# A weight's high part multiplies high and low activations in one 512-column product, and two sums are added afterwards

## The chip, the cores and the metric

The kernel runs on one core of a Trainium2 chip. The metric is the device time of one execution in microseconds (us), lower is better; three executions of the kernel before took 2799.14 to 2809.85 us, median 2800.09 us. TensorE (PE) multiplies matrices into PSUM, VectorE (DVE) and ScalarE (ACT) do the elementwise work and read PSUM, GpSimd (POOL) does a few small operations, and SyncE (SP) issues the loads of the weights. Each engine takes its instructions from a queue of its own, in order.

## The reference

The program is a network of four layers on 256 tokens of width 1024, in 32-bit floats. The first block has two layers, each a mixer, a cross attention to 256 memory tokens and an expert layer (a product key search over two tables of 16384 rows); the second block has two layers, each an attention mixer and a gated feed-forward layer. What matters here are the products of the normalised activations with a weight:

```python
h = h + short_conv_pool_mixer(hn, even_w_in[j], ...)                  # u, gate_c, gate_b, pv = split(hn @ w_in)
q = (h @ wq).reshape(B_, S_, X_HEADS, X_HEAD_DIM)                       # cross attention, both layers
k, v = jnp.split(mem_n @ wkv, 2, axis=-1)
q = (xb @ wq).reshape(PEER_BLOCK, PEER_HEADS, 2, PEER_HALF)             # the experts' query
act = jax.nn.gelu(jnp.einsum('td,ted->te', xb, u[eid]))                 # the experts' first table, u
...
    gu = h @ w_gate_up                                                  # feed-forward, D_FF = 2816
    gate, up = gu[..., :D_FF], gu[..., D_FF:]
    return (jax.nn.silu(gate) * up) @ w_down
```

## The kernel before

**High and low parts.** Every product is made of three. A weight block arrives as 128 x 1024 floats in a tile `raw` (512 KB, one load by SP). ACT copies it, rounded, into `hi` (L114), and DVE subtracts to get `lo` (L117). Activations are split in the same way: `norm_T` fills `xh` and `xl`, each 128 x 8 x 256 (feature chunk by token), on ACT (L281) and DVE (L282). A product is then hi*xh + hi*xl + lo*xh, three matmuls into one PSUM sum (`mm3`, L152 to L154).

**Two forms.** `rows` has the weight as the streamed operand, 512 columns at a time, and sums in the four banks `a0` to `a3`. `columns` has the weight as the loaded operand: for each of 8 feature chunks it loads hi, streams 256 columns of xh, loads hi again, streams 256 columns of xl, loads lo, streams 256 columns of xh. That is 24 matmuls of 256 columns for one block of 128 outputs, in the lower half of one of two banks, `mm0` and `mm1`, which alternate. A bank is used again two blocks later, and has to have been read by then.

**Where `columns` runs.** The experts' first table (names `pu`, 256 blocks, not touched by the change); the experts' queries (`pwq`, 32); the feed-forward's gate and up (`fgu`, 88, that is 44 pairs); queries and keys of the cross attention (`xwq`, 16, and `xwk`, 16); the first mixer (`ein`, 16); the second mixer (`oiq` 6, `ohf` 4, `ohq` 4, `oql` 8); the third (`eqk` 8) and the fourth (`oqk` 10). Nearly always ACT reads the bank and writes the result to SBUF with one instruction, which also applies a scale or a function (Silu at L1311, Sigmoid at L799, scale 1/16 at L419). For `up`, DVE multiplies the bank with the gate straight from PSUM (L1314).

**What sets the order.** The order of each engine's instructions is that of the code. `w` hands out the split block number i, and before it does so it issues the splits up to block i + 2 (three tiles `hi` and three `lo`) and the loads up to block i + 6 (four tiles `raw`). So in the queue of ACT the copy `hi` of block i + 2 stands ahead of what ACT does with the result of block i, and `hi` of block i + 3 stands behind it; likewise `lo` on DVE.

**Names in the diff.** `memory` makes the keys and values of the cross attention and keeps the split memory (`kept`) in DRAM for the second layer; `weave` and `fill` place steps of other work between the blocks, in a fixed rhythm.

Of the kernel before, what the change touches and what calls it, by code (L numbers as in the profile page):

```python
# [20 lines left out]
F32 = mybir.dt.float32  # L21
F32R = mybir.dt.float32r
# [4 lines left out]
OP = mybir.AluOpType  # L27
# [47 lines left out]
class Program:  # L75
    RAW, HL, AHEAD, AHEAD_D = 4, 3, 3, 4

    def __init__(self, nc, tc, ins, out, order, start, stop):
        self.nc, self.tc, self.ins, self.out = nc, tc, ins, out
        self.order = order  # L80
        self.second = None
        self.n_mm = self.n_tp = 0
        self.given2 = [NOTHING] * 5
        self.kept = [NOTHING] * 2
# [71 lines left out]
    def columns(self, ps, name, j, xT, k_n=8):  # L156

        hi, lo = self.w(name, j, 128 * k_n)
        for k in range(k_n):
            s = slice(k * 128, (k + 1) * 128)  # L160
            self.mm3(ps, hi[:, s], lo[:, s], xT[0][:, k, :], xT[1][:, k, :], k == 0, k == k_n - 1)

    def rows(self, name, ks, xT, acc, gain=None):

        ks = list(ks)
        cut = len(ks) - 2
        for k in ks[:cut]:
# [59 lines left out]
    def norm_T(self, src, gain, xn=None, fill=0):  # L227

        hi, lo = [self.act.tile([128, 8, 256], F32R, name=f"x{i}", bufs=1) for i in "hl"]
        done, self.normed = self.normed, 1  # L230
        if xn is not None:
            for _ in self.norm_steps(src, gain, hi, lo, self.ss, xn, self.r, done):
                self.fill(fill)
            return hi, lo
# [5 lines left out]
        return hi, lo  # L240

# [48 lines left out]
    def memory(self, l, pool):  # L290
        nc = self.nc
        mT = [pool.tile([128, 8, 256], F32R, name=f"m{i}") for i in "hl"]
        if l == 0:
# [14 lines left out]
            for k in range(8):  # L308
# [4 lines left out]
                if k % 2:  # L313
                    yield
            self.kept = [self.dram.tile([128, 8, 256], F32, name=f"kept{i}") for i in range(2)]
            for to, m in zip(self.kept, mT):
                nc.gpsimd.dma_start(to, m.bitcast(F32))
        else:
            for m, kept in zip(mT, self.kept):
                nc.gpsimd.dma_start(m.bitcast(F32), kept)  # L320
            yield
# [25 lines left out]
    def conv_pool(self, pool):  # L347
# [18 lines left out]
        for g in range(4):  # L366
            pv = pool.tile([128, 16 + 256], F32, name="pv", bufs=2)
            nc.vector.memset(pv[:, :16], 0.0)
            ps = self.ps_mm()[:, :256]
            self.columns(ps, "ein", 12 + g, xT)  # L370
            nc.scalar.activation(pv[:, 16:], ps, AF.Copy)
            s = pv
# [11 lines left out]
            u = pool.tile([128, 256], F32, name="u", bufs=2)  # L384
            ps = self.ps_mm()[:, :256]
            self.columns(ps, "ein", g, xT)
            nc.scalar.activation(u, ps, AF.Copy)
            yield
# [21 lines left out]
    def xattn(self, l, pool):  # L410
# [101 lines left out]
    def peer(self, l):  # L512
        nc, tc = self.nc, self.tc
        with tc.tile_pool(name=f"peer{l}", bufs=1) as pg:
# [24 lines left out]
            for j in range(16):  # L539
                ps = self.ps_mm()[:, :256]  # L540
# [11 lines left out]
            acc = self.accs()  # L552
            wT = [self.act.tile([128, 8, 256], F32R, name=f"x{i}", bufs=1) for i in "hl"]
            yield from weave(self.peer_down(l, A, wT, acc, 0), self.peer_weigh(l, A, iota, slot, gT, 1), 0.55)
# [161 lines left out]
    def odd_mixer(self, pool):  # L716
# [28 lines left out]
        for j in range(6):  # L745
            ps = self.ps_mm()[:, :256]
            self.columns(ps, "oiq", j, xT)
            nc.scalar.activation(ikw if j == 0 else iqT[:, j - 1, :] if j < 5 else ckvT, ps, AF.Copy)
            if j == 0:
# [43 lines left out]
    def odd_columns(self, pool, xT, H, qlT, lb):  # L793
        nc, v = self.nc, self.nc.vector
        f = H["lf"]
        for j in range(4):
            ps = self.ps_mm()[:, :256]
            self.columns(ps, "ohf", j, xT)
            nc.scalar.activation(f[:, j, :], ps, AF.Sigmoid)  # L799
            v.tensor_scalar(f[:, j, :], f[:, j, :], lb[:, 1, j:j + 1], lb[:, 0, j:j + 1], op0=OP.mult, op1=OP.add)  # L800
# [3 lines left out]
        for j in range(4):  # L804
            ps = self.ps_mm()[:, :256]
            self.columns(ps, "ohq", j, xT)
            nc.scalar.activation(H["hq"][:, j, :], ps, AF.Copy)
            yield
        for name, func in (("hg", AF.Silu), ("hi", AF.Copy)):
# [14 lines left out]
            for j in range(8):  # L824
                ps = self.ps_mm()[:, :256]
                self.columns(ps, "oql", j, xT)
                nc.scalar.activation(qlT[:, j, :], ps, AF.Copy, scale=128.0 ** -0.5)
                yield
# [242 lines left out]
    def even_mixer(self, pool):  # L1071
# [45 lines left out]
        for j in range(8):  # L1117
            ps = self.ps_mm()[:, :256]
            self.columns(ps, "eqk", j, xT)
            nc.scalar.activation((qB if j < 4 else kB)[:, j % 4, :], ps, AF.Copy, scale=0.125 if j < 4 else 1.0)  # L1120
            if j == 0:
# [135 lines left out]
    def window_mixer(self, pool):  # L1257
# [11 lines left out]
        def gemm():  # L1269
            for j in range(10):  # L1270
                ps = self.ps_mm()[:, :256]
                self.columns(ps, "oqk", j, xT)
                nc.scalar.activation((vT, kT)[j] if j < 2 else qT[:, j - 2, :], ps, AF.Copy, scale=1.0 if j < 2 else 0.125)
                if j == 1:
# [27 lines left out]
    def ffn(self, l, pool):  # L1302
# [4 lines left out]
        for j in range(22):  # L1307
            ps = self.ps_mm()[:, :256]
# [3 lines left out]
            ps = self.ps_mm()[:, :256]  # L1312
# [307 lines left out]
```

## Time and profile before

| | |
|---|---|
| median of three executions | 2800.09 us (2799.14 to 2809.85) |
| the profiled execution | 2809.7 us, of it the span 2807.9 us |
| PE busy | 2739.6 us, 98% of the span |
| weight loads on PE | 2465.9 us |
| DVE busy | 1992.6 us, 71% |
| ACT busy | 1346.5 us, 48% |
| chain of work that ended last | PE 92%, DVE 4%, ACT 2% |
| mean rate of DMA | 165 GB/s |

Busy time is read against the span. A matmul's row starts where its columns begin to stream, and its end is modelled and lies beyond the next one's start; so the pace of matmuls is read from start to start, and the idle time in a row tells only of gaps that are longer than that overlap.

### The profile page before, as it was taken

What the parts mean: (1) busy time and instruction counts of PE and PEld (TensorE: products, weight loads), DVE (VectorE), ACT (ScalarE), POOL (GpSimd) and SP (SyncE); (2) the same over time, 40 slices, a digit from 0 to 9 for tenths busy, and PEclk for the clock granted to TensorE, in tenths of its full rate; (3) what the DMA queues carried; (4) which work ended last, traced back from release to release, by engine and by line L of the source; (5) the groups of instructions that cost most, each with busy time, mean ns of one, the idle gap of its engine ahead of it and who ended that gap; (6) DMA issues with size and microseconds to landing.
All of it is one profiled execution on the core that took longest, in us unless ns stands there. A gap on an engine that the chain in (4) does not pass through costs nothing.

```text
span 2807.9 us, 50252 instructions
## 1 busy us (share of the span) xinstructions
PE 2739.6 (98%) x20160; PEld 2465.9 (88%) x20160; DVE 1992.6 (71%) x3692; ACT 1346.5 (48%) x2272; POOL 66.6 (2%) x109
## 2 busy tenths in 40 slices
PE   8999999999999999999999999999999999999998
PEld 7889999998888888978999999888887769977997
DVE  7457898898996566755779889899656545556654
ACT  5455444434444555455544433444455545445543
POOL 2000000000000010100000000000000000000000
PEclk9999999999999999999999999999999989999999
DMA  6645555544555565344555544555555415552454
GB/s 226 212 133 163 186 176 165 167 155 160 166 166 188 194 184 182 123 129 142 166 181 180 173 160 155 163 169 166 187 193 167 165 53 179 183 166 89 158 182 148
DMA packets 127338, 463.32 MB, mean 165 GB/s; under 512 B 14912, under 2 KB 15192, under 8 KB 126336
## 3 DMA queue, kind: packets, MB, share of 16 engines
q1 hardware_dynamic: 122688, 445.31, 48.9%
q0 software_dynamic: 3776, 14.40, 1.7%
q8 instruction: 158, 2.59, 0.4%
q14 instruction: 76, 0.62, 0.1%
q10 hardware_dynamic: 640, 0.40, 0.0%
HBM read 456.64 MB, written 3.34 MB: 164 GB/s over the span
## 4 chain that ended last, share of the span: by engine, by line
PE 92%; DVE 4%; ACT 2%; issue 2%; DMA 1%; POOL 0%; POOLq 0%; DVEq 0%; ACTq 0%; SPq 0%
PE mm L152 16%; PE mm L154 16%; PE mm L153 15%; PE a L152 12%; PE a L154 12%; PE a L153 12%; PE tp L681 3%; DVE lo L117 1%; PE tp L486 1%; PE a L1232 1%; PE a L439 1%; ACT hi L114 1%; PE tp L535 1%; PE a L427 0%; PE a L970 0%
## 5 line engine op out<-in xcount | busy, mean ns | idle before, releaser
L117 DVE TENSOR_TENSOR lo<-raw,hi 128x1024 fp32r<-128x1024 f32 (+2 forms) x847 | 1033.1, 1222 | 614.3 <-ACT hi L114 610.8
L114 ACT ACTIVATE hi<-raw 128x1024 fp32r<-128x1024 f32 (+2 forms) x847 | 890.4, 1051 | 531.3 <-PE a L154 502.1
L152 PE MATMUL mm<-xh,hi 128*128 128x256 f32 x3584 | 1030.3, 287 | 3.3 <-DVE xl L282 2.4
L154 PE MATMUL mm<-xh,lo 128*128 128x256 f32 x3584 | 1019.8, 285 | 7.2 <-DVE lo L117 7.2
L153 PE MATMUL mm<-xl,hi 128*128 128x256 f32 x3584 | 1019.3, 284 | 0.9 <-DVE xl L282 0.9
L154 PEld LDWEIGHTS mm<-xh,lo 128*128 128x128 f32 x3584 | 691.1, 193 | 9.9 <-DVE lo L117 9.9
L152 PEld LDWEIGHTS mm<-xh,hi 128*128 128x128 f32 x3584 | 691.4, 193 | 8.7 <-DVE xl L282 3.8
L153 PEld LDWEIGHTS mm<-xl,hi 128*128 128x128 f32 x3584 | 691.4, 193 | 1.1 <-DVE xl L282 1.1
L152 PE MATMUL a<-hi,xh 128*128 128x512 f32 x1072 | 424.8, 396 | 1.6 <-ACT xh L273 1.6
L154 PE MATMUL a<-hi,xl 128*128 128x512 f32 x1072 | 418.6, 390 | 0.0
L153 PE MATMUL a<-lo,xh 128*128 128x512 f32 x1072 | 417.4, 389 | 0.0
L561 ACT ACTIVATE A<-mm 128x256 f32<-128x256 f32 x256 | 104.5, 408 | 445.7 <-PE mm L154 445.7
L154 PEld LDWEIGHTS a<-hi,xl 128*128 128x128 f32 x1072 | 201.2, 188 | 43.5 <-DVE xl L274 0.3
L152 PEld LDWEIGHTS a<-hi,xh 128*128 128x128 f32 x1072 | 201.5, 188 | 41.4 <-ACT xh L273 2.0
L153 PEld LDWEIGHTS a<-lo,xh 128*128 128x128 f32 x1072 | 201.7, 188 | 40.1
L673 DVE TENSOR_TENSOR go<-o,gT 128x512 bf16<-128x512 bf16 x384 | 140.3, 421 | 4.4
L681 PEld LDWEIGHTS <-o 128*128 128x128 bf16 x3072 | 96.7, 98 | 19.5 <-issue 16.7
L681 PE MATMUL tp<-go,o 128*128 128x64 bf16 x3072 | 111.9, 194 | 0.0
L274 DVE TENSOR_TENSOR xl<-A,xh 128x256 fp32r<-128x256 f32 x256 | 106.6, 418 | 2.0 <-ACT xh L273 2.0
L273 ACT ACTIVATE xh<-A 128x256 fp32r<-128x256 f32 x256 | 106.0, 416 | 0.0
L686 DVE TENSOR_TENSOR A<-tp,A 128x512 f32<-128x512 f32 x128 | 87.7, 685 | 0.0
L668 DVE TENSOR_TENSOR o<-iota,slot 128x1024 bf16<-128x1024 bf16 x128 | 87.6, 684 | 0.0
(463 smaller groups left out, 2548.0 us busy)
## 6 DMA issues: line engine op xcount, KB each, us to landing
raw<-pu SPq DMA_DIRECT2D x256, 512.0 KB, 3.7
raw<-pv SPq DMA_DIRECT2D x256, 512.0 KB, 4.3
raw<-fgu SPq DMA_DIRECT2D x88, 512.0 KB, 3.3
raw<-fdown SPq DMA_DIRECT2D x44, 512.0 KB, 3.4
raw<-pwq SPq DMA_DIRECT2D x32, 512.0 KB, 3.8
raw<-ein SPq DMA_DIRECT2D x16, 512.0 KB, 5.7
raw<-eout SPq DMA_DIRECT2D x16, 512.0 KB, 3.6
raw<-xwk SPq DMA_DIRECT2D x16, 512.0 KB, 4.3
```

The costliest lines, as they stand in the source:

```text
L114: self.nc.scalar.activation(hi, raw, AF.Copy)
L117: self.nc.vector.tensor_tensor(lo, raw, hi.bitcast(F32), OP.subtract)
L152: mm(out, ah, bh, start=start, stop=False)
L153: mm(out, ah, bl, start=False, stop=False)
L154: mm(out, al, bh, start=False, stop=stop)
L273: self.nc.scalar.activation(hi, src, AF.Copy)
L274: self.nc.vector.tensor_tensor(lo, src, hi.bitcast(F32), OP.subtract)
L561: self.nc.scalar.activation(A[:, c // 2, :, c % 2], ps, AF.Gelu_apprx_tanh)
L668: v.tensor_tensor(o2, iota[:, None].to_broadcast([128, 8, 64, 2]), slot[:, 1, t, None].to_broadcast([128, 8, 64, 2]), OP.is_equal)
L673: v.tensor_tensor(go[:, k], o1, gT[:, k, t, None].to_broadcast([128, 8, 32, 2]), OP.mult)
L681: nc.tensor.matmul(ps[:, j, :], o2[:, j].rearrange("p n two -> p (n two)"), go[:, k, j].rearrange("p n two -> p (n two)"), start=k == 0, s ...
L686: v.tensor_tensor(a, prod.pop(i).rearrange("p t (c two) -> p t c two", two=2), a, OP.mult)
```

## The change

A new helper, `columns_to`, takes the place of `columns` and the ACT instruction behind it at twelve places in the code, 200 blocks in all. The high and the low activations now lie side by side in one tile (`xhl`, `mhl`: chunk, part, token), so that the loaded hi streams 512 columns, [xh | xl], into a whole bank: hi*xh in the lower half, hi*xl in the upper. Then lo streams the 256 columns of xh into the lower half. There are 16 matmuls for a block in place of 24, with as many columns streamed. The halves are added outside PE: ACT copies the upper half to SBUF, DVE adds the lower half to it, and where a function or a scale is wanted ACT applies it in a third instruction. The second half of the gate pair (`up`) is now written to a tile by the same two instructions, and multiplied from there. The experts' first table and half of the first mixer (`ein` 4 to 11) keep the old form. The memory is kept in DRAM in two halves by chunk, no longer by part.

```diff
+    def columns_to(self, out, name, j, xT, func=AF.Copy, scale=1.0):
+        hi, lo = self.w(name, j)
+        ps = self.ps_mm()
+        for k in range(8):
+            s = slice(k * 128, (k + 1) * 128)
+            self.nc.tensor.matmul(ps, hi[:, s], xT[2][:, k].rearrange("p i t -> p (i t)"), start=k == 0, stop=False)
+            self.nc.tensor.matmul(ps[:, :256], lo[:, s], xT[0][:, k, :], start=False, stop=k == 7)
+        self.nc.scalar.activation(out, ps[:, 256:], AF.Copy)
+        self.nc.vector.tensor_tensor(out, ps[:, :256], out, OP.add)
+        if func != AF.Copy or scale != 1.0:
+            self.nc.scalar.activation(out, out, func, scale=scale)
...
-        hi, lo = [self.act.tile([128, 8, 256], F32R, name=f"x{i}", bufs=1) for i in "hl"]
+        both = self.act.tile([128, 8, 2, 256], F32R, name="xhl", bufs=1)
+        hi, lo = both[:, :, 0], both[:, :, 1]
...
-            ps = self.ps_mm()[:, :256]
-            self.columns(ps, f"xwq{l}", j, xT)
-            nc.scalar.activation(qT[:, j, :], ps, AF.Copy, scale=1.0 / 16.0)
+            self.columns_to(qT[:, j, :], f"xwq{l}", j, xT, scale=1.0 / 16.0)
...
-                ps = self.ps_mm()[:, :256]
-                self.columns(ps, f"pwq{l}", j, xT)
-                nc.scalar.activation(q[:, j % 4], ps, AF.Copy)
+                self.columns_to(q[:, j % 4], f"pwq{l}", j, xT)
...
-            ps = self.ps_mm()[:, :256]
-            self.columns(ps, f"fgu{l}", 2 * j, xT)
             g = pool.tile([128, 256], F32, name="gate", bufs=2)
-            nc.scalar.activation(g, ps, AF.Silu)
-            ps = self.ps_mm()[:, :256]
-            self.columns(ps, f"fgu{l}", 2 * j + 1, xT)
-            v.tensor_tensor(g, ps, g, OP.mult)
+            self.columns_to(g, f"fgu{l}", 2 * j, xT, AF.Silu)
+            u = pool.tile([128, 256], F32, name="up", bufs=2)
+            self.columns_to(u, f"fgu{l}", 2 * j + 1, xT)
+            v.tensor_tensor(g, u, g, OP.mult)
             self.hilo(YT[0][:, j, :], YT[1][:, j, :], g)
```

The first place is ACT's queue in the first feed-forward layer, one gate and up pair and the start of the next, before the change. `hi` are the copies of coming weight blocks, `gate` is the Silu of a bank, `fYT0` the high part of the pair's product.

```order
L114 ACTIVATE hi_26755<-raw_26625 128x1024
L1311 ACTIVATE gate_26785<-mm1_26754 128x256
L114 ACTIVATE hi_26788<-raw_26658 128x1024
L273 ACTIVATE fYT0_26015<-gate_26785 128x256
L114 ACTIVATE hi_26822<-raw_26692 128x1024
L1311 ACTIVATE gate_26852<-mm1_26821 128x256
```

The same place on ACT with the change (L172 is the copy of a bank's upper half, L175 the Silu, `up` the new tile):

```order
L172 ACTIVATE gate_25658<-mm1_25665 128x256
L175 ACTIVATE gate_25658<-gate_25658 128x256
L114 ACTIVATE hi_25686<-raw_25578 128x1024
L172 ACTIVATE up_25685<-mm0_25692 128x256
L288 ACTIVATE fYT0_25320<-gate_25658 128x256
L114 ACTIVATE hi_25715<-raw_25607 128x1024
L172 ACTIVATE gate_25714<-mm1_25721 128x256
L175 ACTIVATE gate_25714<-gate_25714 128x256
```

The Silu, which read the bank that PE had filled, now reads what DVE wrote, and the next block's `hi` still stands behind it.

The second place is DVE's queue at that pair, before the change:

```order
L117 TENSOR_TENSOR lo_26756<-raw_26625,hi_26755 128x1024
L117 TENSOR_TENSOR lo_26789<-raw_26658,hi_26788 128x1024
L1314 TENSOR_TENSOR gate_26785<-mm0_26787,gate_26785 128x256
L274 TENSOR_TENSOR fYT1_26016<-gate_26785,fYT0_26015 128x256
L117 TENSOR_TENSOR lo_26823<-raw_26692,hi_26822 128x1024
```

And with the change (L173 adds a bank's lower half):

```order
L117 TENSOR_TENSOR lo_25660<-raw_25551,hi_25659 128x1024
L173 TENSOR_TENSOR gate_25658<-mm1_25665,gate_25658 128x256
L117 TENSOR_TENSOR lo_25687<-raw_25578,hi_25686 128x1024
L173 TENSOR_TENSOR up_25685<-mm0_25692,up_25685 128x256
L1307 TENSOR_TENSOR gate_25658<-up_25685,gate_25658 128x256
L289 TENSOR_TENSOR fYT1_25321<-gate_25658,fYT0_25320 128x256
L117 TENSOR_TENSOR lo_25716<-raw_25607,hi_25715 128x1024
L173 TENSOR_TENSOR gate_25714<-mm1_25721,gate_25714 128x256
```

Two additions stand between the subtractions `lo`, and each empties a bank; before, DVE had one instruction there that read a bank.

The third place is ACT's queue in the first layer's cross attention queries, before the change:

```order
L419 ACTIVATE xqT_1533<-mm1_1534 128x256
L114 ACTIVATE hi_1563<-raw_1422 128x1024
L419 ACTIVATE xqT_1533<-mm0_1562 128x256
L114 ACTIVATE hi_1595<-raw_1440 128x1024
L419 ACTIVATE xqT_1533<-mm1_1594 128x256
```

And with the change, where DVE's addition of the same block stands between L172 and L175:

```order
L172 ACTIVATE xqT_1417<-mm1_1420 128x256
L175 ACTIVATE xqT_1417<-xqT_1417 128x256
L114 ACTIVATE hi_1440<-raw_1307 128x1024
L172 ACTIVATE xqT_1417<-mm0_1446 128x256
L175 ACTIVATE xqT_1417<-xqT_1417 128x256
L114 ACTIVATE hi_1466<-raw_1325 128x1024
```

One scaled copy has become a copy and, two queues further, a scaling, with the next `hi` behind both.

## Rows read from the trace of the kernel before

**Rows 1.** The page, part 1: busy us, share of span, instructions, by engine.
```profile
PE 2739.6 (98%) x20160; PEld 2465.9 (88%) x20160; DVE 1992.6 (71%) x3692; ACT 1346.5 (48%) x2272; POOL 66.6 (2%) x109
```

**Rows 2.** Windows, one stretch a row: us, busy by engine, clock, DMA.
```profile
core 0: us, PE busy (x) PEld busy (x) DVE busy (x) ACT busy (x) POOL busy (x), PEclk, DMA share, GB/s
...
1112.00:1145.00 33.00, 32.01 (x257) 31.79 (x257) 27.10 (x45) 16.86 (x27) 2.85 (x3) 0.95 0.38 123
...
2230.00:2318.00 88.00, 84.19 (x375) 57.05 (x376) 40.55 (x133) 43.65 (x124) 1.13 (x2) 0.89 0.18 57
...
2318.00:2440.00 122.00, 122.00 (x1015) 122.00 (x1015) 70.45 (x88) 58.75 (x88) 0.00 (x0) 1.00 0.56 181
```

**Rows 3.** Timeline, PE in `fgu`, first and last of 36: start, us, instruction.
```profile
2319.78 0.28 PE L154 MATMUL mm<-xh,lo 128*128 128x256 f32 x1
...
2323.98 0.28 PE L153 MATMUL mm<-xl,hi 128*128 128x256 f32 x1
```

**Rows 4.** Timeline, PE in `rows`, first and last of 19.
```profile
999.75 0.39 PE L152 MATMUL a<-hi,xh 128*128 128x512 f32 x1
...
1003.83 0.39 PE L152 MATMUL a<-hi,xh 128*128 128x512 f32 x1
```

**Rows 5.** Timeline, DVE in `fgu`; in brackets idle time before, and releaser.
```profile
2322.20 1.23 DVE L117 TENSOR_TENSOR lo<-raw,hi 128x1024 fp32r<-128x1024 f32 x1 [1.42 <-ACT hi L114]
2323.70 0.42 DVE L1314 TENSOR_TENSOR gate<-mm,gate 128x256 f32<-128x256 f32 x1 [0.27 <-PE mm L154]
2324.61 0.43 DVE L274 TENSOR_TENSOR fYT<-gate,fYT 128x256 fp32r<-128x256 f32 x1 [0.48 <-ACT fYT L273]
2325.56 1.22 DVE L117 TENSOR_TENSOR lo<-raw,hi 128x1024 fp32r<-128x1024 f32 x1 [0.52 <-ACT hi L114]
```

**Rows 6.** Timeline, ACT in the same stretch.
```profile
2321.12 1.05 ACT L114 ACTIVATE hi<-raw 128x1024 fp32r<-128x1024 f32 x1
2324.16 0.42 ACT L273 ACTIVATE fYT<-gate 128x256 fp32r<-128x256 f32 x1 [1.99 <-DVE gate L1314]
2324.48 1.04 ACT L114 ACTIVATE hi<-raw 128x1024 fp32r<-128x1024 f32 x1
```

**Rows 7.** Timeline, DVE in the first mixer.
```profile
59.36 0.42 DVE L381 TENSOR_TENSOR pd<-ws,rcnt 128x256 f32<-128x256 f32 x1
59.82 0.42 DVE L382 TENSOR_TENSOR pd<-pd,pv 128x256 f32<-128x256 f32 x1
```

**Rows 8.** Timeline, DVE in `pwq`: one period.
```profile
230.27 1.23 DVE L117 TENSOR_TENSOR lo<-raw,hi 128x1024 fp32r<-128x1024 f32 x1 [0.51 <-ACT hi L114]
...
231.41 0.29 DVE L506 MAX8 A<-A 128x8 f32<-128x128 f32 x1
...
232.79 0.28 DVE L510 FIND_INDEX8 A<-A 128x8 uint32<-128x128 f32 x1
...
233.59 1.23 DVE L117 TENSOR_TENSOR lo<-raw,hi 128x1024 fp32r<-128x1024 f32 x1 [0.51 <-ACT hi L114]
```

**Rows 9.** Timeline, PE at the start of the first cross attention.
```profile
164.94 1.89 PE L427 MATMUL a<-KT,xqT 128*128 128x256 f32 x8
167.07 1.13 PE L427 MATMUL a<-KT,xqT 128*128 128x256 f32 x4 [0.25 <-ACT ap L464]
```

**Rows 10.** Timeline, ACT at the same place.
```profile
165.13 0.38 ACT L419 ACTIVATE xqT<-mm 128x256 f32<-128x256 f32 x1 [1.55 <-PE mm L154]
166.46 0.47 ACT L464 ACTIVATE ap<-a,ast 128x256 f32<-128x256 f32 x1 [0.94 <-DVE ast L463]
```

**Rows 11.** Timeline, PE at the fourth mixer's first logits.
```profile
2520.43 0.92 PE L1286 MATMUL a<-kT,sqT 64*128 64x128 f32 x4 [0.47 <-ACT sqT L1273]
```

**Rows 12.** The chain that ended last, second mixer: start us, us, what.
```profile
1053.38 11.03 DMA raw<-ohf
```

**Rows 13.** Waits of PE, 1040 to 1150 us: total us, times, longest.
```profile
PE tp L842 <- ACT ckv L767: 2.1, 1, 2.1
```

More of the change, by code (lines that the diff above doesn't have):

```diff
@@ L83, in __init__ @@
         self.given2 = [NOTHING] * 5
-        self.kept = [NOTHING] * 2
+        self.kept = NOTHING
         self.asked = []
@@ L233, in norm_T @@
                 self.fill(fill)
-            return hi, lo
+            return hi, lo, both
         self.n_norm += 1
@@ L239, in norm_T @@
                 self.fill(fill)
-        return hi, lo
+        return hi, lo, both
     def norm_steps(self, src, gain, hi, lo, ss, xn, r, done=1):
@@ L291, in memory @@
         nc = self.nc
-        mT = [pool.tile([128, 8, 256], F32R, name=f"m{i}") for i in "hl"]
+        both = pool.tile([128, 8, 2, 256], F32R, name="mhl")
+        mT = both[:, :, 0], both[:, :, 1], both
         if l == 0:
@@ L314, in memory @@
                     yield
-            self.kept = [self.dram.tile([128, 8, 256], F32, name=f"kept{i}") for i in range(2)]
-            for to, m in zip(self.kept, mT):
-                nc.gpsimd.dma_start(to, m.bitcast(F32))
-        else:
-            for m, kept in zip(mT, self.kept):
-                nc.gpsimd.dma_start(m.bitcast(F32), kept)
+            self.kept = self.dram.tile([128, 8, 2, 256], F32, name="kept")
+            for i in range(2):
+                nc.gpsimd.dma_start(self.kept[:, 4 * i:4 * i + 4], both[:, 4 * i:4 * i + 4].bitcast(F32))
+        else:
+            for i in range(2):
+                nc.gpsimd.dma_start(both[:, 4 * i:4 * i + 4].bitcast(F32), self.kept[:, 4 * i:4 * i + 4])
             yield
@@ L325, in memory @@
         for j in range(8):
-            ps = self.ps_mm()[:, :256]
-            self.columns(ps, f"xwk{l}", j, mT)
-            nc.scalar.activation(KT[:, j, :], ps, AF.Copy)
+            self.columns_to(KT[:, j, :], f"xwk{l}", j, mT)
             yield
@@ L368, in conv_pool @@
             nc.vector.memset(pv[:, :16], 0.0)
-            ps = self.ps_mm()[:, :256]
-            self.columns(ps, "ein", 12 + g, xT)
-            nc.scalar.activation(pv[:, 16:], ps, AF.Copy)
+            self.columns_to(pv[:, 16:], "ein", 12 + g, xT)
             s = pv
@@ L384, in conv_pool @@
             u = pool.tile([128, 256], F32, name="u", bufs=2)
-            ps = self.ps_mm()[:, :256]
-            self.columns(ps, "ein", g, xT)
-            nc.scalar.activation(u, ps, AF.Copy)
+            self.columns_to(u, "ein", g, xT)
             yield
@@ L539, in peer @@
             for j in range(16):
-                ps = self.ps_mm()[:, :256]
-                self.columns(ps, f"pwq{l}", j, xT)
-                nc.scalar.activation(q[:, j % 4], ps, AF.Copy)
+                self.columns_to(q[:, j % 4], f"pwq{l}", j, xT)
                 if j:
@@ L552, in peer @@
             acc = self.accs()
-            wT = [self.act.tile([128, 8, 256], F32R, name=f"x{i}", bufs=1) for i in "hl"]
+            both = self.act.tile([128, 8, 2, 256], F32R, name="xhl", bufs=1)
+            wT = both[:, :, 0], both[:, :, 1]
             yield from weave(self.peer_down(l, A, wT, acc, 0), self.peer_weigh(l, A, iota, slot, gT, 1), 0.55)
@@ L745, in odd_mixer @@
         for j in range(6):
-            ps = self.ps_mm()[:, :256]
-            self.columns(ps, "oiq", j, xT)
-            nc.scalar.activation(ikw if j == 0 else iqT[:, j - 1, :] if j < 5 else ckvT, ps, AF.Copy)
+            self.columns_to(ikw if j == 0 else iqT[:, j - 1, :] if j < 5 else ckvT, "oiq", j, xT)
             if j == 0:
@@ L796, in odd_columns @@
         for j in range(4):
-            ps = self.ps_mm()[:, :256]
-            self.columns(ps, "ohf", j, xT)
-            nc.scalar.activation(f[:, j, :], ps, AF.Sigmoid)
+            self.columns_to(f[:, j, :], "ohf", j, xT, AF.Sigmoid)
             v.tensor_scalar(f[:, j, :], f[:, j, :], lb[:, 1, j:j + 1], lb[:, 0, j:j + 1], op0=OP.mult, op1=OP.add)
@@ L804, in odd_columns @@
         for j in range(4):
-            ps = self.ps_mm()[:, :256]
-            self.columns(ps, "ohq", j, xT)
-            nc.scalar.activation(H["hq"][:, j, :], ps, AF.Copy)
+            self.columns_to(H["hq"][:, j, :], "ohq", j, xT)
             yield
@@ L824, in odd_columns @@
             for j in range(8):
-                ps = self.ps_mm()[:, :256]
-                self.columns(ps, "oql", j, xT)
-                nc.scalar.activation(qlT[:, j, :], ps, AF.Copy, scale=128.0 ** -0.5)
+                self.columns_to(qlT[:, j, :], "oql", j, xT, scale=128.0 ** -0.5)
                 yield
@@ L1117, in even_mixer @@
         for j in range(8):
-            ps = self.ps_mm()[:, :256]
-            self.columns(ps, "eqk", j, xT)
-            nc.scalar.activation((qB if j < 4 else kB)[:, j % 4, :], ps, AF.Copy, scale=0.125 if j < 4 else 1.0)
+            self.columns_to((qB if j < 4 else kB)[:, j % 4, :], "eqk", j, xT, scale=0.125 if j < 4 else 1.0)
             if j == 0:
@@ L1270, in gemm @@
             for j in range(10):
-                ps = self.ps_mm()[:, :256]
-                self.columns(ps, "oqk", j, xT)
-                nc.scalar.activation((vT, kT)[j] if j < 2 else qT[:, j - 2, :], ps, AF.Copy, scale=1.0 if j < 2 else 0.125)
+                self.columns_to((vT, kT)[j] if j < 2 else qT[:, j - 2, :], "oqk", j, xT, scale=1.0 if j < 2 else 0.125)
                 if j == 1:
```

2 lines of the change are left out of this document (removed).

## The prediction

> **What bounds the kernel now.** I read the busy line first: PE is busy 98% of the span, DVE 71%, ACT less than half [rows 1]. Then the windows by stage: in the first feed-forward layer PE has no idle time at the full clock, while DVE works 70 of 122 us and ACT 59 [rows 2]. So I went to the pace of the matmuls, from start to start, which idle times don't show. The 256-column matmuls of the gate and up blocks come every 4.20 us / 35 = 120.0 ns [rows 3], the 512-column ones of `rows` every 4.08 us / 18 = 226.7 ns [rows 4]. The reader is to see two things in this pair: 256 more columns cost 106.7 ns, which is 0.417 ns a column, and what is left, 120.0 - 106.7, is 13.3 ns for each matmul whatever its width. Last I read the queues of DVE and ACT at one pair of blocks [rows 5, 6], because the change gives both of them work between a block's end and the reuse of its bank.
>
> **What PE gains.** A block has 24 matmuls, 24 x 120.0 = 2.880 us. Afterwards it has 8 x (226.7 + 120.0) = 2.773 us: as many columns, eight matmuls fewer, 0.107 us saved. For 200 blocks that is 21.3 us, if PE remains what everything waits for. No row shows a 512-column matmul of this form between 256-column ones; the bounds are no gain (0) and these 13.3 ns, and I take the latter since both widths show it.
> A rule to weigh here: the Trainium skill, "TensorE: Matmul & The Clock Gate", section "Back-to-back issue gap", gives columns / 2.4 ns plus 2.5 ns for a matmul at the full clock. The slope agrees with the rows, the fixed part does not: 13.3 ns were measured here, and the rows decide. By the page the 1600 matmuls saved would be worth 4 us, and my total would come out 17 us higher.
>
> **What the other queues pay, in the feed-forward layers.** For each pair DVE gets two additions more and ACT one copy, some 0.4 us each [rows 5]; by busy time that fits easily. But the queues are in order, which the trace shows: ACT sat idle for 1.99 us in front of `fYT0`, waiting for DVE's product, and only behind it came the next `hi` [rows 6]. With the change ACT waits for DVE twice in a pair (Silu for the first addition, `fYT0` for the product), and DVE stands behind ACT's `hi` twice (each `lo`, with an addition behind it). The steps close to a loop, which must run once for each pair. From start to start:
> addition of the gate to Silu 0.46 (as the product at 2323.70 to `fYT0` at 2324.16) [rows 5, 6]; Silu to the next `hi` 0.32 (2324.16 to 2324.48) [rows 6]; `hi` to its `lo` 1.08 (2321.12 to 2322.20) [rows 5, 6]; `lo` to the addition of `up` behind it 1.14 (230.27 to 231.41) [rows 8]; addition to the product, which needs it, 0.46 (59.36 to 59.82) [rows 7]; product to `fYT0` 0.46; `fYT0` to the next `hi` 0.32; `hi` to `lo` 1.08; `lo` to the next gate's addition 1.14. The sum is 6.46 us. PE needs 2 x 2.773 = 5.55 us for the pair. Before, the part of this loop from the product by way of `fYT0`, one `hi`, the Silu, another `hi` and its `lo` back to the product needed no step of DVE in between and was well under PE's 5.76 us.
> So the loop is the bound, and PE waits for its banks. At first there is slack: an addition starts about 0.65 us after its block's last column (0.19 until ACT starts, 164.94 to 165.13 [rows 9, 10], and 0.45 for ACT's copy until DVE starts, as 2324.16 to 2324.61 [rows 5, 6]) and frees the bank 0.47 later; PE wants it back 2.77 us after the block's end. That leaves 1.65 us, and each pair loses 6.46 - 5.55 = 0.91 us of it, so PE waits from the third or fourth pair on. With 18 of 22 pairs waiting, a layer's gate stage takes 22 x 5.55 + 18 x 0.91 = 138.4 us against 22 x 5.76 = 126.7: +11.7 us. At its end ACT runs some 4.5 us behind PE, and the third block of `fdown` gets its `lo` about 1.2 us late. Two layers: 2 x 12.9 = +25.8 us. An error of 0.1 us in the loop moves this by 3.6.
>
> **The other stages.**
> Cross attention queries (2 x 8): the scaled copy becomes copy, addition, scaling. Its loop is 0.46 + 0.32 + 1.08 + 1.14 = 3.00 us against PE's 2.77, so it slips 0.23 for each block, 1.6 in eight, just the slack: PE saves its 0.85. But the last scaling then ends 3.0 us after the last block, where the first softmax began 1.52 after it (164.94 to 166.46 [rows 9, 10]), and PE already waits there for that softmax, 0.25 us [rows 9]. So 1.5 is lost for 0.85 gained: +0.65 each, +1.3 (bounds -1.7 and +3).
> Experts' queries (32): plain copies, no loop through ACT. DVE's period is 3.32 us with 0.51 idle [rows 8]; 2.81 + 0.42 = 3.23 against PE's 3.32 - 0.107 = 3.21. Level, with the bank's slack above to spare: -3.4 (bounds -3.4 and +2). The cover here is those 0.5 us of DVE, and it is used up.
> Memory keys (16), plain copies with both engines half idle: -1.7 (bounds -1.7 and 0).
> First mixer (8): -0.85 of PE, but two additions (0.84) in the last of its four groups, where the DVE rows follow each other without a gap [rows 7]: 0 (bounds -0.85 and +2).
> Third mixer (8): -0.85, and +0.8 (0.46 + 0.32, as above) for the first block's eviction, behind which ACT empties transposes: 0 (bounds -0.85 and +2).
> Fourth mixer (10): -1.07; its first logits wait 0.47 for ACT already [rows 11], and the addition and scaling come on top, 0.8; some 0.7 later on. +0.4 (bounds -1.1 and +4).
> Second mixer (22): PE's share is -2.35. Six blocks lie ahead of a load that took 11 us and is itself on the chain [rows 12], so their 0.64 comes back; the first Sigmoid block has a copy more, 0.3, in front of what PE waits 2.1 us for [rows 13]; and around 1112 to 1145 us DVE is at 82% [rows 2] and gets 0.4 for each block of 4 us, in loops with ACT that no row prices: I take 2.4. +1 (bounds -2.35 and +8).
> Sum: 25.8 + 1.3 - 3.4 - 1.7 + 0 + 0 + 0.4 + 1 = +23.4 us. On the profiled execution's 2809.7 us (span and 1.8 us around it) that is 2833.1. That execution lies 9.6 us above the median shown; on the median, 2800.09 + 23.4 = 2823.5 us.
>
> **Rivals.**
> PE stays the bound everywhere (the other side): 2800.1 - 21.3 = 2778.8, or 2788 if only the feed-forward loop doesn't bind (-18.8 for it: 2 x -4.7 there, the other terms as above, -2.4). For it: DVE and ACT would be busy only some 70% and 60% of those stages. Against it: it needs a loop below 5.55 us, 0.91 less than nine read steps give. It decides from there. Chance 0.06, both together.
> The loop binds, but shorter, about 6.0 us, since steps overlap that I read as serial: 16 pairs x 0.45 = 7.2, less 4.7, + 1.2 at the end, for each layer +3.7; with the others 2800.1 + 7.4 - 2.4 = 2805. Each step is a measured pair of starts, so I hold it for less likely. Chance 0.13.
> The loops bind elsewhere too: the DVE queue of the experts' queries slips, and the second and fourth mixers pay near their upper bounds. +3.4 + 5 + 3: 2835. For it speaks the level balance in the experts' queries. Chance 0.15.
> The gaps in PE cost it its clock: where PE had gaps, in the third mixer's attention, the granted clock was 0.89 [rows 2]. At 0.89 a pair takes PE 5.55 / 0.89 = 6.2 us, still under the loop; below 0.86 it would be the bound, at 0.7 (7.9 us) 36 x 1.5 = 53 us more, 2876. Chance 0.02.
>
> **How the numbers follow.** My forecast has 0.64, with a range of its own of 2812 to 2834 (loop +-0.1 us, 3.6; half of the other bounds). For 8 in 10 I reach to the shorter loop below and to the other loops above: 2804 to 2838. Within 0.5%, what a measurement of this kernel can tell from no change, is 2786 to 2814. Slower: 0.64 + 0.15 + 0.02, less 0.02 from the forecast's lower edge, 0.79. Same: the shorter loop, part of the milder rival and that edge, 0.16. Faster: 0.05.
>
> **What would show it.** Each step in turn: in the feed-forward windows matmul pairs of 0.347 us, PE busy below 90% and waits of PE at L170 for DVE's L173, in sum 15 to 20 us a layer, starting at the third or fourth pair; a period of 6.4 to 6.5 us for a pair; ACT's L175 waiting for DVE. In the experts' queries a period of 3.21 us and no waits. At the first softmax of the cross attentions PE waiting 1.5 us longer. PE instructions down by 1600. I am wrong if the pair's period is 5.55 us, or if a matmul of 512 columns here takes more than 227 ns.

## The result

The changed kernel took 2847.63 us (four executions, 2841.52 to 2850.63) against 2802.08 us (2799.14 to 2809.85): ratio 1.0156, 95% interval 1.0136 to 1.0175. Slower was forecast, and the largest part for the reason forecast; but the loss is 45.5 us where I had put 23.4, and the time lies outside the range of 2804 to 2838.

The page of the changed kernel, the line that answers to [rows 1]:

```profile
PE 2745.4 (96%) x18560; PEld 2372.1 (83%) x18560; DVE 2061.2 (72%) x3892; ACT 1386.3 (49%) x2400; POOL 66.6 (2%) x109
```

The 1600 matmuls are gone, and the span is 37.8 us longer all the same. The windows of the two gate and up stages after the change, for the 122 us row of [rows 2]:

```profile
2326.00:2466.00 140.00, 132.83 (x703) 107.17 (x704) 87.17 (x135) 73.38 (x135) 0.00 (x0) 1.00 0.53 162
2635.00:2775.00 140.00, 132.58 (x702) 106.99 (x702) 87.17 (x135) 73.67 (x136) 0.00 (x0) 1.00 0.54 162
```

A stage that took 127 us takes 140. The granted clock is full, DVE and ACT are busy 62% and 52%, so by these columns nothing is short of anything. ACT's timeline in that stage, the columns as in [rows 6]:

```profile
2379.86 0.42 ACT L288 ACTIVATE fYT<-gate 128x256 fp32r<-128x256 f32 x1 [1.82 <-DVE gate L1307]
2380.19 1.04 ACT L114 ACTIVATE hi<-raw 128x1024 fp32r<-128x1024 f32 x1
2381.14 0.37 ACT L172 ACTIVATE gate<-mm 128x256 f32<-128x256 f32 x1
2382.86 0.42 ACT L175 ACTIVATE gate<-gate 128x256 f32<-128x256 f32 x1 [1.36 <-DVE gate L173]
2383.18 1.04 ACT L114 ACTIVATE hi<-raw 128x1024 fp32r<-128x1024 f32 x1
2384.13 0.36 ACT L172 ACTIVATE up<-mm 128x256 f32<-128x256 f32 x1
2386.31 0.42 ACT L288 ACTIVATE fYT<-gate 128x256 fp32r<-128x256 f32 x1 [1.82 <-DVE gate L1307]
```

From `fYT` to `fYT` it is 6.45 us, where the sum of nine steps had 6.46, and each of the nine, read from start to start in these rows and the next, is within 0.01 us of what was summed. ACT waits twice in it, 1.82 and 1.36 us, both times for DVE. DVE, at the same time:

```profile
2381.26 1.22 DVE L117 TENSOR_TENSOR lo<-raw,hi 128x1024 fp32r<-128x1024 f32 x1 [0.52 <-ACT hi L114]
2382.41 0.42 DVE L173 TENSOR_TENSOR gate<-mm,gate 128x256 f32<-128x256 f32 x1
2384.26 1.23 DVE L117 TENSOR_TENSOR lo<-raw,hi 128x1024 fp32r<-128x1024 f32 x1 [1.43 <-ACT hi L114]
2385.40 0.42 DVE L173 TENSOR_TENSOR up<-mm,up 128x256 f32<-128x256 f32 x1
2385.85 0.42 DVE L1307 TENSOR_TENSOR gate<-up,gate 128x256 f32<-128x256 f32 x1
```

DVE waits for ACT's `hi`, and ACT for DVE's addition: each idles for the other, and PE's bank comes free behind both (PE's waits, 2326 to 2467 us):

```profile
PE mm L170 <- DVE gate L173: 7.0, 19, 0.4
```

Nineteen waits, from the fourth of 22 pairs on, as foretold. Their 7.0 us are less than the 12 us lost, since a matmul's modelled end covers part of each gap.

**The ledger.** Each stage's length, from the start of its first matmul to that of the next stage's, in the two profiles (us, after minus before; the experiments below show which of these go with the granted clock):

| stage | forecast | measured |
|---|---|---|
| two feed-forward layers | +25.8 | +27.3 |
| second mixer, with the second layer's memory keys | +0.2 | +8.6 |
| third mixer | 0 | +2.1 |
| first mixer, with the first memory keys | -0.9 | +1.3 |
| cross attentions | +1.3 | +1.2 |
| fourth mixer | +0.4 | +1.1 |
| experts (queries and first table) | -3.4 | -3.6 |
| sum | +23.4 | +38.0 |

### The profile page after: what moved, and what is told of

Its sections match the earlier page's. It is cut to its first block, busy times and chain, and to the rows that moved or that the text cites. A ratio compares the mean times of both kernels' runs of the same rounds, so it can differ in the third digit from the quotient of the medians.

```text
span 2845.7 us, 47324 instructions
## 1 busy us (share of the span) xinstructions
PE 2745.4 (96%) x18560; PEld 2372.1 (83%) x18560; DVE 2061.2 (72%) x3892; ACT 1386.3 (49%) x2400; POOL 66.6 (2%) x109
## 4 chain that ended last, share of the span: by engine, by line
PE 79%; DVE 9%; ACT 6%; issue 4%; DMA 1%; POOL 0%; ACTq 0%; POOLq 0%; DVEq 0%; SPq 0%
PE a L152 12%; PE a L153 11%; PE a L154 11%; PE mm L152 9%; PE mm L154 9%; PE mm L153 9%; PE mm L170 5%; DVE lo L117 4%; ACT hi L114 4%; PE tp L688 3%; PE mm L171 3%; PE tp L494 1%; DVE gate L1307 1%; DVE gate L173 1%; PE a L1229 1%
## 5 line engine op out<-in xcount | busy, mean ns | idle before, releaser
L152 PE MATMUL mm<-xhl,hi 128*128 128x256 f32 x2112 | 604.4, 286 | 2.4 <-DVE u L173 2.1
L154 PE MATMUL mm<-xhl,lo 128*128 128x256 f32 x2112 | 598.9, 284 | 6.6 <-DVE lo L117 6.6
L153 PE MATMUL mm<-xhl,hi 128*128 128x256 f32 x2112 | 597.6, 283 | 0.0
L170 PE MATMUL mm<-xhl,hi 128*128 128x512 f32 x1472 | 543.1, 410 | 21.3 <-DVE gate L173 14.0
L152 PE MATMUL a<-hi,xhl 128*128 128x512 f32 x1072 | 424.5, 396 | 1.6 <-ACT xhl L288 1.6
L154 PE MATMUL a<-hi,xhl 128*128 128x512 f32 x1072 | 418.2, 390 | 0.0
L153 PE MATMUL a<-lo,xhl 128*128 128x512 f32 x1072 | 417.1, 389 | 0.0
L171 PE MATMUL mm<-xhl,lo 128*128 128x256 f32 x1472 | 413.7, 281 | 0.0
L154 PEld LDWEIGHTS mm<-xhl,lo 128*128 128x128 f32 x2112 | 405.1, 192 | 9.1 <-DVE lo L117 9.1
L152 PEld LDWEIGHTS mm<-xhl,hi 128*128 128x128 f32 x2112 | 405.4, 192 | 3.6 <-DVE u L173 2.5
L153 PEld LDWEIGHTS mm<-xhl,hi 128*128 128x128 f32 x2112 | 405.4, 192 | 0.1
L170 PEld LDWEIGHTS mm<-xhl,hi 128*128 128x128 f32 x1472 | 278.4, 189 | 113.0 <-DVE gate L173 26.4
L171 PEld LDWEIGHTS mm<-xhl,lo 128*128 128x128 f32 x1472 | 280.1, 190 | 0.0
L154 PEld LDWEIGHTS a<-hi,xhl 128*128 128x128 f32 x1072 | 201.2, 188 | 43.5 <-DVE xhl L289 0.3
L152 PEld LDWEIGHTS a<-hi,xhl 128*128 128x128 f32 x1072 | 201.4, 188 | 41.6 <-ACT xhl L288 2.0
L153 PEld LDWEIGHTS a<-lo,xhl 128*128 128x128 f32 x1072 | 201.6, 188 | 40.1
L688 PEld LDWEIGHTS <-o 128*128 128x128 bf16 x3072 | 96.7, 98 | 19.5 <-issue 16.7
```

Source lines behind the costliest of these rows:

```text
L152: mm(out, ah, bh, start=start, stop=False)
L153: mm(out, ah, bl, start=False, stop=False)
L154: mm(out, al, bh, start=False, stop=stop)
L170: self.nc.tensor.matmul(ps, hi[:, s], xT[2][:, k].rearrange("p i t -> p (i t)"), start=k == 0, stop=False)
L171: self.nc.tensor.matmul(ps[:, :256], lo[:, s], xT[0][:, k, :], start=False, stop=k == 7)
L688: nc.tensor.matmul(ps[:, j, :], o2[:, j].rearrange("p n two -> p (n two)"), go[:, k, j].rearrange("p n two -> p (n two)"), start=k == 0, s ...
```

## The experiments

**1. The loop in the feed-forward layers.** One line of the changed kernel's helper: the split of the block three ahead goes in front of what waits for DVE.

```diff
-        self.nc.vector.tensor_tensor(out, ps[:, :256], out, OP.add)
+        self._split(lambda: self.nc.vector.tensor_tensor(out, ps[:, :256], out, OP.add))
```

> The changed kernel, with the split of the block three ahead issued between the copy of a bank's upper half and the scaling or Silu: the same instructions, ACT's next copy no longer behind the instruction that waits for DVE. Theory of the loop (ACT and DVE wait for each other once around for each feed-forward pair): the pair's period falls from 6.45 us to PE's own 5.6, both gate stages lose 15 us each, the attentions' first softmax comes 1 us earlier each; 2810 us (2804 to 2818). Rival, the work itself (more instructions on ACT and DVE, whatever their order): no change, 2848 us. Rival, PE is slower in the new form: no change either.

2835.13 us, ratio 1.0117 (1.0097 to 1.0137): only 12.5 us better, a miss by the total. By stage it is two opposite results. The two gate stages fell from +12.3 and +13.1 us to -4.6 and -2.2 against the kernel before. Their windows, and ACT's timeline in the first:

```profile
2340.20:2463.40 123.20, 123.20 (x707) 108.56 (x706) 88.44 (x136) 74.60 (x137) 0.00 (x0) 0.99 0.60 187
2639.30:2764.10 124.80, 124.80 (x705) 107.89 (x706) 88.54 (x136) 74.48 (x137) 0.00 (x0) 1.00 0.59 185
```

```profile
2399.96 0.42 ACT L288 ACTIVATE fYT<-gate 128x256 fp32r<-128x256 f32 x1 [1.63 <-DVE gate L1307]
2400.28 0.37 ACT L172 ACTIVATE gate<-mm 128x256 f32<-128x256 f32 x1
2400.55 1.05 ACT L114 ACTIVATE hi<-raw 128x1024 fp32r<-128x1024 f32 x1
2401.50 0.41 ACT L175 ACTIVATE gate<-gate 128x256 f32<-128x256 f32 x1
2402.55 0.38 ACT L172 ACTIVATE up<-mm 128x256 f32<-128x256 f32 x1 [0.65 <-PE mm L171]
2402.89 1.06 ACT L114 ACTIVATE hi<-raw 128x1024 fp32r<-128x1024 f32 x1
2405.58 0.42 ACT L288 ACTIVATE fYT<-gate 128x256 fp32r<-128x256 f32 x1 [1.62 <-DVE gate L1307]
```

The Silu no longer waits, for the `hi` ahead of it covers DVE's addition; the pair takes 5.62 us; PE has no idle time, with the same instructions on ACT and DVE in another order. So the loop is shown, and neither their work nor PE's pace was the bound here. But other stages lost: the latent queries of the second mixer went from +3.2 to +11.3 us against before, the fourth mixer from +1.1 to +8.7. In the mixers the `hi` now stands ahead of scalings that other work waits for (PE's waits for DVE's `kk` among the latent queries rose from 4.0 to 7.3 us). That is not all of it, for the granted clock fell too: to 0.85 among the latent queries, where the changed kernel had 0.95, and to 0.50 from 2582 to 2594 us in the fourth mixer, behind its queries, where 5.3 of the 8.7 us lie. The two parts can't be told apart from this run.

**2. The feed-forward layers in the old form** (the rest changed).

```diff
-            self.columns_to(g, f"fgu{l}", 2 * j, xT, AF.Silu)
...
+            self.columns(ps, f"fgu{l}", 2 * j, xT)
+            nc.scalar.activation(g, ps, AF.Silu)
```

> The changed kernel with the two feed-forward layers in the old form. By the ledger of the two profiles the feed-forward layers cost 27.2 us of the 37.8: 2820 us. If the cost were spread over all 200 blocks alike, 44% of it would go: 2828 us.

2817.84 us, ratio 1.005 (1.0034 to 1.0066): 29.8 us of the 45.5 go with 44% of the blocks. The layers' share is that of the ledger; spread evenly it would have been 20.

**3. The second mixer in the old form.**

```diff
-            self.columns_to(f[:, j, :], "ohf", j, xT, AF.Sigmoid)
+            ps = self.ps_mm()[:, :256]
+            self.columns(ps, "ohf", j, xT)
+            nc.scalar.activation(f[:, j, :], ps, AF.Sigmoid)
...
```

> The changed kernel with the second mixer's 22 blocks in the old form. By the ledger the second mixer with its memory keys costs 8.6 us, so 2839 us, and PE's waits for the hq bank (2.3 us) and for kk (4.0 us) fall back to 0 and 1.0. If it was the memory keys alone or the earlier stages' delay: no change, 2848 us.

2841.9 us, ratio 1.0131 (1.0107 to 1.0155), and in the profile the first 14 blocks' stretch is back from +3.8 to +0.3, the latent queries' from +3.2 to 0. PE's waits for the hq bank and for `kk` fell to 0 and 1.0 us, as expected. The memory keys and what follows keep their +1.6; it is no firm figure, for the same form there came out at -0.1 in two later kernels (best and pairs, at the full clock). So most of the ledger's 8.6 us is in these 22 blocks. Which of two causes, a loop with ACT or DVE's full queue, the next two tell.

**4. The scale applied on the way out of the bank.** No instruction behind the addition any more, except Silu and Sigmoid; DVE's work is unchanged.

```diff
-        self.nc.scalar.activation(out, ps[:, 256:], AF.Copy)
-        self.nc.vector.tensor_tensor(out, ps[:, :256], out, OP.add)
-        if func != AF.Copy or scale != 1.0:
-            self.nc.scalar.activation(out, out, func, scale=scale)
+        self.nc.scalar.activation(out, ps[:, 256:], AF.Copy, scale=scale)
...
+            self.nc.vector.scalar_tensor_tensor(out, ps[:, :256], scale, out, op0=OP.mult, op1=OP.add)
+        if func != AF.Copy:
+            self.nc.scalar.activation(out, out, func)
```

> The changed kernel, with a scale applied while the halves leave the bank: ACT copies the upper half with the scale, DVE multiplies the lower half by it and adds, so that the attentions' queries and the second mixer's latent queries have no third instruction and ACT waits for DVE nowhere there. DVE's work is unchanged. Theory of the loop for the second mixer: its latent queries fall from +3.2 us to about -0.5 against the kernel before, the cross attentions to -0.5 each, the third and fourth mixers lose 1 us each: 2838 us. Theory of DVE's load in the second mixer (the additions stand in a queue that is full there, whoever waits): +3.2 stays within 0.7, so 2842 us.

2837.02 us, ratio 1.0128 (1.0114 to 1.0143). The latent queries fell from +3.2 to -0.2 us, the cross attentions from +0.8 and +0.4 to -0.5 and -0.9, the third mixer's queries from +2.3 to -0.4, the fourth mixer from +1.1 to +0.1. ACT's waits in the changed kernel at the latent queries (total, times, longest), and then with the scale folded in:

```profile
ACT qlT L175 <- DVE qlT L173: 9.9, 7, 2.4
ACT qlT L172 <- PE mm L171: 6.8, 4, 2.9
```

```profile
ACT qlT L172 <- PE mm L171: 16.1, 7, 4.2
```

DVE does as many additions; ACT waits no longer for them. But the granted clock of the latent queries rose as well. Their windows in the kernel before, in the changed one, with the scale folded in, and in the old form at the full clock (the run best, below):

```profile
1111.61:1144.49 32.88, 31.89 (x258) 31.71 (x258) 26.77 (x44) 16.52 (x27) 2.85 (x3) 0.95 0.39 127
1114.80:1150.88 36.08, 32.08 (x194) 28.07 (x194) 29.25 (x51) 17.97 (x32) 2.84 (x3) 0.95 0.37 116
1116.07:1148.71 32.64, 30.28 (x195) 26.61 (x194) 29.14 (x51) 16.55 (x27) 2.84 (x3) 1.00 0.40 129
1108.30:1139.93 31.63, 30.64 (x258) 30.34 (x258) 26.70 (x44) 16.52 (x27) 2.85 (x3) 1.00 0.43 133
```

At 0.95 the new form costs 3.2 us, at 1.00 with the scale folded 1.0. So ACT's wait was some 2.2 us of the 3.2; the other 1.0 is still there, with PE's waits for DVE's `kk` at 2.4 us (1.0 before, 4.0 with the change), and whether DVE's load makes it is open. The third mixer's queries hold such a shift too: PE's transposes behind the first block cost 1.6 us more than before in the changed kernel and 0.4 more here, but the seven blocks behind them took 21.0 us at a clock of 0.94 and 19.5 at 1.00, and 21.1 at 0.92 in a later kernel with the scale folded (best3).

**5. The four Sigmoid blocks alone in the old form** (the edit is the one shown under 3).

> The changed kernel with the second mixer's four Sigmoid blocks in the old form. The stretch of its first 14 blocks took 52.2 us before and 56.0 or 59.0 with the change, the difference of 3 us going with the granted clock. If the chain bank, copy, addition, Sigmoid, DVE's next step is what costs there: 52.5 to 53.5 us. If the plain additions of the ten other blocks stand in DVE's full queue: 55 us or more.

The stretch of 14 blocks: 52.3 us, +0.2 against before, at the same granted clock. (One execution, 2841.22 us.) The windows of the kernel before and of this run:

```profile
1043.98:1096.13 52.15, 48.92 (x373) 46.40 (x371) 33.09 (x73) 29.22 (x57) 9.56 (x16) 0.95 0.68 217
1046.50:1098.81 52.31, 48.71 (x292) 41.95 (x291) 36.09 (x82) 29.14 (x57) 9.58 (x16) 0.95 0.69 210
```

Ten plain blocks in the new form cost nothing there; the four Sigmoids cost all. DVE in the changed kernel, at the second and third of them:

```profile
1074.76 0.42 DVE L173 TENSOR_TENSOR lf<-mm,lf 128x256 f32<-128x256 f32 x1 [2.06 <-ACT lf L172]
1075.66 0.41 DVE L803 TENSOR_SCALAR lf<-lf,lb 128x256 f32<-128x256 f32 x1 [0.48 <-ACT lf L175]
...
1078.48 1.22 DVE L117 TENSOR_TENSOR lo<-raw,hi 128x1024 fp32r<-128x1024 f32 x1
1079.93 0.42 DVE L173 TENSOR_TENSOR lf<-mm,lf 128x256 f32<-128x256 f32 x1 [0.23 <-ACT lf L172]
1080.85 0.41 DVE L803 TENSOR_SCALAR lf<-lf,lb 128x256 f32<-128x256 f32 x1 [0.49 <-ACT lf L175]
```

For each block DVE stands waiting twice, for the copy and for the Sigmoid, and what stands behind in its queue comes later. PE waited 2.3 us for a bank of the next four blocks (`hq`) that DVE had not yet emptied; with the Sigmoid blocks in the old form that wait is gone.

**6. Both kernels once more with a profile**, the code unchanged.

> The kernel before, once more with a profile. The two profiles differ by 37.8 us, the medians by 45.5 us. If the first profiled execution of the kernel before was a slow one (2809.7 us against a median of 2802), this profile shows 2800 us and one or a few stages shorter; if a profile itself costs the kernel before some 8 us, it shows 2809 again.

> The changed kernel once more with a profile. The third mixer's attention took 109 us at a granted clock of 0.89 in some profiles and 103 us at 0.95 in others. If that state belongs to the kernel, this profile shows 109 us again and the ledger of the first; if it falls by chance in each execution, it may show 103 us, and the spread of each kernel's times (2799 to 2810, 2841 to 2851) is of its size.

The kernel before: 2803.25 us in the median, ratio 1.0002 (0.9991 to 1.0014), its profiled execution 2809.0 again, with the first ledger within 1.5 us at each stage. The changed kernel: 2844.36 us, its profiled execution 2845.3; but two stages had moved. In the first profile (the 14 blocks, then the third mixer's attention; the clock is the third figure from the end):

```profile
1043.37:1099.32 55.95, 48.58 (x261) 39.68 (x259) 37.73 (x86) 30.48 (x61) 9.60 (x16) 0.95 0.63 197
2214.00:2323.16 109.16, 103.22 (x446) 69.39 (x445) 51.03 (x170) 52.54 (x146) 0.57 (x1) 0.89 0.24 73
```

In the second:

```profile
1043.49:1102.68 59.19, 51.62 (x260) 42.01 (x259) 38.35 (x87) 30.52 (x61) 9.67 (x16) 0.90 0.61 192
2217.27:2320.41 103.14, 97.23 (x446) 65.93 (x445) 50.84 (x171) 52.08 (x146) 0.57 (x1) 0.95 0.25 77
```

The 14 blocks take 3.2 us more, the third mixer's attention 6.0 us less, with the granted clock of the stretch and the same instructions. In the attention either clock came in either form: 0.89 in both profiles of the kernel before and in the first of the changed kernel, 0.95 in the second. So a difference of this size there is the clock's. In the 14 blocks it is not by chance alone: of the five profiles with the four Sigmoids in the new form four show 58.8 to 59.2 us at 0.90 or 0.91, and only the first 55.9 at 0.95; all eight with them in the old form show 52.1 to 52.6 at 0.95 to 0.97. There the lower clock came only with the change, and the price of the Sigmoids is 3.8 us or, more often, 7.

The gap between 45.5 us (medians) and 37.8 (profiles) goes mostly with the clock, for each execution's mean granted clock was noted. Of 60 executions of the kernel before, 17 at 0.993 took 2799.6 us in the mean, 10 at 0.990 took 2806.4, and 2 at 0.988 took 2810.6. Six of the changed kernel took 2841.5 us at 0.992, 2843.4 and 2845.3 at 0.991, 2847.5 at 0.990, 2847.7 at 0.989 and 2850.6 at 0.988. At one and the same clock the change costs 39 to 42 us. The first profile of the kernel before was one of its slow-clocked executions (0.988), while its median lies at 0.992. Whether the change itself draws the lower clocks, six executions can't tell.

**7. What is worth keeping.** First the new form only for the experts' queries, the memory keys and the feed-forward layers, these with the split ahead (`columns_to(..., early=True)` does the edit of experiment 1 there alone).

> The new form only for the experts' queries, the memory's keys and the feed-forward layers, there with the split issued ahead of the Silu; all else in the old form. By the ledger: feed-forward -4.6 and -2.2, experts' queries -1 each, memory keys -0.5: 9 us under the kernel before, 2793 us. If the stages' gains don't add up because later ones give them back through the clock or other waits: 2802 us.

2798.37 us, ratio 0.9984 (0.9974 to 0.9993). Then with the scaled queries of the cross attention:

> As best, and the cross attentions' queries in the new form with the scale applied on the way out of the bank. If the loop through ACT was what ate their gain, they bring 0.5 us each more, 2792 us; if it was DVE or the later softmax, they lose 0.5 each, 2794 us.

2797.37 us, ratio 0.998 (0.9971 to 0.9988). These queries gained 0.6 us in each layer against the run before, which had them in the old form; the two totals can't be told apart. Then the first of the two with another order of matmuls:

```diff
+        for k2 in range(0, 8, 2):
+            for k in (k2, k2 + 1):
...
+                self.nc.tensor.matmul(ps, hi[:, s], xT[2][:, k].rearrange("p i t -> p (i t)"), start=k == 0, stop=False)
+            for k in (k2, k2 + 1):
...
+                self.nc.tensor.matmul(ps[:, :256], lo[:, s], xT[0][:, k, :], start=False, stop=k == 7)
```

> As best, with the matmuls of two chunks reordered: 512, 512, 256, 256 columns in place of 512, 256, 512, 256. The changed kernel's pairs come at 346.7 ns in some stretches and 353.3 ns in others. If the longer pace is the price of changing between widths, it halves: all stretches at 346.7 or 350 ns a chunk, and some 3 us less than best. If it is a state of the queue that has nothing to do with widths, both paces remain and the time is that of best.

2797.2 us, ratio 0.9979 (0.9969 to 0.9988). In the feed-forward layers a chunk takes 348.4 ns, in both layers and evenly, where it took 353.4 and 354.1 in best, with the single order; the gate stages are at -4.1 and -3.8 us against before, not -2.3 and -2.2. The total, 1.2 us lower, can't be told from that of best. That the alternation makes the longer pace is not shown: in the same single order the first gate stage of experiment 1 ran at 346.7 ns throughout (its window is above), and the first cross attention's queries ran at 353.3 ns in one profile of the changed kernel and at 346.7 in the other. With the pairs the longer pace came in none of four gate stages (this run and the next); what sets it stays open. Last, all together:

> All that has paid so far in one kernel: matmuls in pairs of chunks, scales applied on the way out of the bank, the feed-forward's splits issued ahead of the Silu; the first mixer and the second mixer's first 14 blocks in the old form. Sum of the ledger: feed-forward -7.8, experts' queries -2, cross attention queries -1.5, memory keys -1.2, latent queries and third mixer -0.6: 13 us under the kernel before, 2789 us. If the gains don't add up: 2797, as best2 and pairs.

2796.32 us, ratio 0.9977 (0.9968 to 0.9986). This beats both kernels, by 6 us over the kernel before, half of the 13 summed up; best2 and pairs it can't be told from. By the profiles the span did fall by 12.8 us, but they were taken at mean clocks of 0.988 (before) and 0.990, and the third mixer's attention fell at a higher one; at one and the same clock the executions differ by 7 to 9 us.

## Why the prediction was right, and where it was wrong

- **The loop in the feed-forward layers**: right, and shown. 6.46 us forecast, 6.45 read; +25.8 forecast, +27.3 read; undone by an order of instructions alone (experiment 1), and by the old form (2). Two of its signs read otherwise: PE is busy 95% there, not below 90%, and the page's waits are 7.0 us a layer, not 15 to 20. From start to start the gate stage takes 140.0 us where 352 pairs of matmuls at 353.3 ns take 124.4, so 15.6 us are lost.
- **The gain of a block on PE**, "8 x (226.7 + 120.0) = 2.773 us": too good in most stretches. A pair of matmuls comes at 346.7 ns in the first memory keys, but at 353.3 through the cross attention queries and much of the feed-forward in the first profile of the changed kernel. PE here, and then in the first cross attention's queries in the second profile:

```profile
2379.88 0.40 PE L170 MATMUL mm<-xhl,hi 128*128 128x512 f32 x1
2380.12 0.28 PE L171 MATMUL mm<-xhl,lo 128*128 128x256 f32 x1
...
2382.00 0.40 PE L170 MATMUL mm<-xhl,hi 128*128 128x512 f32 x1
```

```profile
154.95 0.39 PE L170 MATMUL mm<-xhl,hi 128*128 128x512 f32 x1
155.18 0.28 PE L171 MATMUL mm<-xhl,lo 128*128 128x256 f32 x1
...
157.03 0.39 PE L170 MATMUL mm<-xhl,hi 128*128 128x512 f32 x1
```

  Six pairs in 2.12 us are 353.3 ns, six in 2.08 us 346.7. At the longer pace a block saves 0.053 us, half. In the feed-forward the loop hid that; with the loop cut, the two gate stages gained 2.3 and 2.2 us in best, and 4.6 and 2.2 in experiment 1, where 4.7 had been put. The sign "a matmul of 512 columns here takes more than 227 ns" came true even at the shorter pace: the 256-column matmul starts 0.23 us after the 512-column one (230 ns in the mean of such a stretch), and the next pair 0.12 us after that. The fixed 13.3 ns was read in streams of one width, and I carried it over to a mixed one.
- **The second mixer**, "in loops with ACT that no row prices: I take 2.4", and "the first Sigmoid block has a copy more, 0.3": this is the step that failed. The total of +1 was +7.0 for its own blocks in the first profile, +10.3 in the second. I had priced the loop of the cross attention's scaled copies from rows and did not do it for the same form here, where DVE has other work in the loop: 3.2 us for eight scaled blocks, some 2.2 of it ACT's wait (experiment 4), and 3.6 for four Sigmoids at one and the same clock (5). And I put the clock at nothing here; the rival "the gaps in PE cost it its clock" looked at the feed-forward, where the clock stayed at 0.99 to 1.00, while among the 14 blocks it fell to 0.90, for another 3 us (6).
- **Third and first mixer**: the third, at +2.1, just above my upper bound, the first inside it. In the third's queries 1.2 us of the +2.3 were the wait for the first block's eviction, which I had put at 0.8; the rest went with the clock, 0.94 there (experiment 4). The stretch of the first mixer's 16 blocks read +1.1 to +1.5 in five of the seven profiles with the new form, -0.1 and +2.7 in the other two; in the old form it was within 0.1 us of before, but for one profile at the full clock, -1.5. Why it costs that is open.
- **Cross attentions and experts' queries**: the sums are right, +1.2 for +1.3, and -3.6 for -3.4, both partly by luck. In the first cross attention the queries saved 0.24 us, not 0.85, and the softmax cost 1.1, not 1.5; in the second the kernel before ran its queries at a clock of 0.965, without which the two layers are at +1.8. The -3.6 holds a shift of some 1.5 us that the kernel before shows between its own two profiles. The period of the experts' queries is 3.21 us, as forecast, but it had been 3.29 in the mean, not 3.32.
- **The step from profile to median**: I took the 9.6 us between the profiled execution and the median for something that stays. It went with that execution's clock (0.988), and the changed kernel's profiled execution lies at its median. The time missed the forecast of 2823.5 by 24.1 us: 14.4 in the stages, of which the second mixer has 8.4, and 9.7 in this step. With either of the two put right the time would have come out at 2838 to 2839, the upper end of the range.
- **Rivals**: PE as the bound everywhere, and the loop of 6.0 us, fell with the 6.45 us period. Of "the loops bind elsewhere too" (2835, chance 0.15) only the second mixer's part came true, near the upper bound put there; the experts' queries didn't slip, and the fourth mixer paid 1.1.
- **Two sums of the prediction**: the 2788 us beside the first rival follow with 2 x -4.7 = -9.4 for the feed-forward, not with the -18.8 written there. And the 17 us by which the total was to come out higher with a smaller fixed part count all 200 blocks, though the loop hides most of what PE saves in the feed-forward's 88; for the other 112 it is 9.7.

## What to carry to other kernels

When an eviction by one engine becomes a chain over two in-order queues (copy, add, function), sum the steps from start to start around the loop, including what stands behind each waiting instruction; busy shares of 60% say nothing about it. Do that sum at every place of the form, above all where the queue holds other work, and cut the loop by order (issue the next independent work ahead of the wait) or by folding the last step into the others. Before a few microseconds of a stage are put down to a change, compare the granted clock of the two stretches, and of the two executions before their times are subtracted; then ask whether the lower clock comes in both forms or only with the change.

## What the runs showed of the hardware

A matmul costs 13.3 ns beside its columns at the full clock in streams of one width (120.0 ns at 256 columns, 226.7 at 512); in an alternating stream the pair costs 346.7 or 353.3 ns, each over long stretches, and the same stretch of one and the same kernel came at either in two executions; with widths alternating half as often it was 348.4 a chunk. The third mixer's attention takes 103 or 109 us at granted clocks of 0.95 or 0.89, in executions of one and the same kernel. Over whole executions of the kernel before, a mean granted clock of 0.993 went with 2799.6 us and one of 0.988 with 2810.6.
